# One transformer-like layer on one core: queries and keys split at the input projection, attention's output halves added by a transfer

## The chip, the cores and the metric

The kernel runs on 1 core of one Trainium2 chip. The metric is the device time of one execution in microseconds (us). Engines are named as in the profile: PE is TensorE's matmul, PEld its weight load, DVE is VectorE, ACT is ScalarE, POOL is GpSimd, SP is SyncE, which here only issues transfers.

## The reference, cut to what matters

One layer on x (2048 x 1024): a normalisation, one input projection of 2816 columns, two groups of heads (sliding-window attention with sinks, and a gated linear recurrence), an output projection, cross-attention into 256 memory tokens, and a SwiGLU network. The change touches the projection's first 640 columns and the attention:

```python
u = rms_norm(h, g_mix_pre[l])
z = u @ w_in[l]
qa, ka, va, qh, fh, ih, gh = jnp.split(z, IN_SPLITS, axis=-1)     # 512, 128, 128, 512, 512, 512, 512
...
s = jnp.einsum('bnqhgd,bnkhd->bhgqk', qc, kband).astype(jnp.float32) * (Dh ** -0.5)
s = jnp.where(valid[None, :, None, None, None, :], s, NEG_INF)
sink = jnp.broadcast_to(sinks.astype(jnp.float32).reshape(1, 1, Hkv, G, 1, 1), (B, NC, Hkv, G, CHUNK, 1))
p = jax.nn.softmax(jnp.concatenate([s, sink], axis=-1), axis=-1)[..., :L]
o = jnp.einsum('bnhgqk,bnkhd->bnqhgd', p.astype(v.dtype), vband)
```

There are 8 query heads and 2 key and value heads of 64, a window of 128 frames in chunks of 64, and Dh ** -0.5 = 0.125.

## The kernel before

**Precision.** Every f32 product is made of parts: an operand x becomes hi, x rounded to f32r by a copy, and lo = x - hi. A product is three matmuls, hi*hi + hi*lo + lo*hi (`mm3`, L156 to L158). A split is a copy on ACT (L999) or POOL (L1001) and a subtraction on DVE (L1002).

**Stages.** First (0 to about 265 us), `in_first` reads x, normalises it, transposes it and multiplies it with the input projection's weights for the first 1024 frames. It goes over pairs of column blocks of 128. Pairs are either plain (`in_block` with plain, columns 4, 5 and 0, 1; three matmuls for each product, result in tiles zp, copied by ACT L654 and stored) or made by a scheme with seven products for a 2 x 2 block (`seven`, L1162 to L1164), whose products are copied out of PSUM to tiles part (ACT L1177) and added by DVE (L661) into a tile z of two columns. Tiles zp, th and part come from one pool with three buffers (tag "part"). The blocks 2 and 3 are the first that go through the seven products. The steps run in the order 1, 5, 6, 3, 7, 2, 4; the steps 1, 6, 7 and 4 use one PSUM bank, so the copy of step 1's product must be done before step 6 can begin. z goes to DRAM as z_d, columns by frames; columns 0 to 511 are the queries, 512 to 639 the keys, 640 to 767 the values. At the end `in_first` also multiplies the first pair (columns 4, 5) for frames 1024 to 2047; the other columns of these frames are made by `in_cols`, one column of 128 at a time, beside the attention.

**Attention** (about 265 to 610 us) goes over 16 tiles of 128 frames, each in two methods. `swa_front` loads the queries of four heads twice into qd, rows 0 to 63 and 64 to 127 (64 rows are one head's dimension), so that the upper half can become hi and the lower half lo of the same numbers: ACT L787 scales by -0.125, DVE L788 makes the lower half the difference. Keys are loaded twice into kr and split by POOL (kh, L1001) and DVE (kl, L1002). The products with the queries are L822 and L823: 128 rows carry hi and lo of q at once. DVE L827 adds the mask and takes the minimum (w_mn), ACT L831 the exponential, POOL L834 and L837 the sink's part of the sum (w_se, w_dn), DVE L839 the reciprocal (w_rd) and L842 the scaling of the rows S. `swa_back`, a tile later, transposes S on PE (L856), splits it (pth by ACT L860, ptl by DVE L861), and multiplies with the stacked v (vst: 64 columns hi, 64 columns lo; L865, L866). The bank's lower and upper 64 rows then hold two halves of the output, which are added: ACT L869 copies one into ys, DVE L870 adds the other. SP stores ys into y_d[n, :, 0:512]. ys has one buffer. Beside this run the recurrence's tiles (`hgrn`) and the remaining columns of the projection, both of which put matmuls between those of attention. Everything from about 640 us on is the same in both kernels.

**Order.** The program is written as generators that take turns; a scheduler with a simulated timeline sets the order of instructions on each engine, and each engine then runs its own in that order. An instruction that waits holds up everything behind it on its engine. All transfers of this part are issued by SP. Transfers that add into DRAM, issued by POOL, are there in the network's last stage already (`add_to`, L1566, y_d<-row).

## Time and profile before

| | |
|---|---|
| median of 3 runs | 2534.37 us (2533.18 to 2536.8) |
| profiled execution, span | 2530.8 us, 34134 instructions |
| PE busy | 2496.8 us, 99% |
| DVE busy | 1794.5 us, 71% |
| ACT busy | 1262.1 us, 50% |
| POOL busy | 375.2 us, 15% |
| DMA | 470.07 MB in 305133 packets, 186 GB/s in the mean |

The profiled execution's own time isn't given beside its span; the median stands 3.57 us above the span, for what lies around it. An engine's busy time counts its instructions; idle time is put down to what released the instruction that ended it. "x32" counts instructions, "us to landing" is from a transfer's issue to the end of its write. A slow clock of PE shows as PEclk below 1.00. PE is nearly always busy, so what counts is what PE waits for, stage by stage.

### The profile page before, as it was taken

Reading aid. Unit: us, or ns where it says so; the run is one execution under the profiler, and the core shown is the slowest. Engines: PE = TensorE matmul, PEld = TensorE weight load, DVE = VectorE, ACT = ScalarE, POOL = GpSimd, SP = SyncE. Lnnn points to the kernel's source line nnn. Section 1 sums busy time; section 2 is a strip of 40 time slices with the busy share of each in tenths; the row PEclk is TensorE's granted clock in tenths of the full one; section 3 lists DMA queues with packets and bytes.
Section 4 is the critical chain, followed back from the end, with each engine's and each line's share of the span. In section 5 each row is a group of like instructions: output and inputs, shape, how many; then the busy total and the mean of one; then the engine's idle time right before and its main releaser. Section 6 shows DMA issues by size and latency. Waiting matters only on the chain.

```text
span 2530.8 us, 34134 instructions
## 1 busy us (share of the span) xinstructions
PE 2496.8 (99%) x11942; PEld 2087.0 (82%) x11942; DVE 1794.5 (71%) x2863; ACT 1262.1 (50%) x2627; POOL 375.2 (15%) x540
## 2 busy tenths in 40 slices
PE   9999999999999999999999999999999999999998
PEld 8878888888987888878878888888888888888886
DVE  8785488986557889988866655576566557664766
ACT  5453466655565576566753333353333335443543
POOL 4231344321401111112200000000000000000022
PEclk9999999999999999999999999999999999999999
DMA  6455645673887996758944322254354334565776
GB/s 199 152 167 177 176 145 156 199 248 114 276 311 261 299 335 196 251 175 256 346 161 168 135 77 93 80 192 154 129 208 167 117 130 155 182 178 112 228 173 153
DMA packets 305133, 470.07 MB, mean 186 GB/s; under 512 B 21440, under 2 KB 193472, under 8 KB 304960
## 3 DMA queue, kind: packets, MB, share of 16 engines
q1 hardware_dynamic: 298912, 445.86, 52.7%
q0 software_dynamic: 6048, 22.02, 5.1%
q8 instruction: 94, 1.54, 0.3%
q14 instruction: 79, 0.65, 0.1%
HBM read 301.09 MB, written 166.72 MB: 185 GB/s over the span
## 4 chain that ended last, share of the span: by engine, by line
PE 84%; DVE 6%; DMA 4%; ACT 3%; issue 2%; POOL 1%; SPq 0%; DVEq 0%; POOLq 0%; ACTq 0%
PE psm L1164 23%; PE psm L1162 23%; PE psm L1163 22%; PE psg L156 2%; PE psg L158 2%; PE psg L157 2%; DVE T L1002 1%; DVE S L1002 1%; DMA raw<-in_wo_x_dram 1%; ACT junk L1533 1%; SPq L75 0%; DMA row<-h_d 0%; PE pss L156 0%; PE pss L157 0%; PE pss L158 0%
## 5 line engine op out<-in xcount | busy, mean ns | idle before, releaser
L1162 PE MATMUL psm<-T,S 128*128 128x512 f32 x2680 | 1034.3, 391 | 10.3 <-ACT part L1177 5.6
L1163 PE MATMUL psm<-T,S 128*128 128x512 f32 x2680 | 1042.9, 390 | 1.5 <-DVE T L1002 1.4
L1164 PE MATMUL psm<-T,S 128*128 128x512 f32 x2680 | 1029.8, 390 | 3.7 <-DVE S L1002 3.7
L1162 PEld LDWEIGHTS psm<-T,S 128*128 128x128 f32 x2680 | 503.2, 188 | 122.5 <-ACT part L1177 9.9
L1164 PEld LDWEIGHTS psm<-T,S 128*128 128x128 f32 x2680 | 503.4, 188 | 111.1 <-DVE S L1002 6.7
L1163 PEld LDWEIGHTS psm<-T,S 128*128 128x128 f32 x2680 | 503.5, 188 | 107.2 <-DVE T L1002 3.7
L999 ACT ACTIVATE S<-sum 128x512 fp32r<-128x512 f32 (+1 forms) x370 | 224.3, 620 | 375.7 <-PE psm L1164 274.2
L1002 DVE TENSOR_TENSOR S<-sraw,S 128x512 fp32r<-128x512 f32 (+1 forms) x315 | 212.1, 680 | 237.2 <-ACT S L999 234.1
L1177 ACT ACTIVATE part<-psm 128x512 f32<-128x512 f32 x285 | 168.8, 597 | 260.4 <-PE psm L1164 241.9
L1002 DVE TENSOR_TENSOR S<-sum,S 128x512 fp32r<-128x512 f32 (+1 forms) x388 | 258.5, 675 | 45.2 <-ACT S L999 41.2
L999 ACT ACTIVATE S<-sraw 128x512 fp32r<-128x512 f32 (+1 forms) x300 | 184.4, 618 | 109.2 <-PE psm L1164 107.3
L1566 POOL DMA_DIRECT2D y_d<-row x16 | 14.1, 879 | 1077.0 <-DVE row L1748 1026.1
L1002 DVE TENSOR_TENSOR T<-row,T 128x1024 fp32r<-128x1024 f32 (+1 forms) x112 | 131.0, 1186 | 27.7 <-ACT T L999 25.7
L156 PE MATMUL psg<-u,whi 128*128 128x512 f32 x320 | 127.6, 399 | 1.3 <-DVE z L730 1.3
L158 PE MATMUL psg<-u,wlo 128*128 128x512 f32 x320 | 127.4, 399 | 0.0
L157 PE MATMUL psg<-u,whi 128*128 128x512 f32 x320 | 127.4, 398 | 0.0
L1533 ACT ACTIVATE junk<-row 128x512 f32<-128x512 f32 x160 | 99.7, 625 | 43.5 <-DVE row L1555 21.2
L999 ACT ACTIVATE T<-row 128x1024 fp32r<-128x1024 f32 (+1 forms) x112 | 113.4, 1032 | 7.3 <-DMA row<-in_w_down_dram 2.8
L1699 DVE TENSOR_TENSOR row<-psm,part 128x512 f32<-128x512 f32 x66 | 44.1, 688 | 71.3 <-PE psm L1164 71.3
L1002 DVE TENSOR_TENSOR wlo<-raw,whi 128x1024 fp32r<-128x1024 f32 x52 | 64.0, 1232 | 41.4 <-ACT whi L999 30.6
L1748 DVE TENSOR_TENSOR row<-psm,part 128x512 f32<-128x512 f32 x72 | 49.2, 689 | 49.3 <-PE psm L1164 49.1
L831 ACT ACTIVATE S<-S,w_mn 128x256 f32<-128x256 f32 (+1 forms) x128 | 63.1, 496 | 41.4 <-DVE w_mn L827 41.0
(355 smaller groups left out, 3541.3 us busy)
## 6 DMA issues: line engine op xcount, KB each, us to landing
sraw<-in_w_gate_dram SPq DMA_DIRECT2D x44, 512.0 KB, 3.8
sraw<-in_w_up_dram SPq DMA_DIRECT2D x44, 512.0 KB, 3.7
hid_d<-row SPq DMA_DIRECT2D x44, 512.0 KB, 2.7
sraw<-hid_d SPq DMA_DIRECT2D x32, 512.0 KB, 4.4
sraw<-in_w_in_dram SPq DMA_DIRECT2D x48, 256.0 KB, 3.8
z_d<-pair SPq DMA_DIRECT2D x20, 512.0 KB, 3.3
raw<-in_w_in_dram SPq DMA_DIRECT2D x20, 512.0 KB, 4.6
z_d<-z SPq DMA_DIRECT2D x20, 512.0 KB, 3.8
```

Source lines behind the costliest of these rows:

```text
L156: nc.tensor.matmul(ps, ah, bh, start=(i == 0), stop=False)
L157: nc.tensor.matmul(ps, ah, bl, start=False, stop=False)
L158: nc.tensor.matmul(ps, al, bh, start=False, stop=(i == n - 1))
L831: nc.scalar.activation(s[:, r, o:], s[:, r, o:], AF.Exp, bias=mn[:, i:i + 1], scale=-1.0, accum_out=den[:, i:i + 1])
L999: self.nc.scalar.activation(hi, raw, AF.Copy)
L1002: self.nc.vector.tensor_tensor(lo, raw, f32(hi), ALU.subtract)
L1162: nc.tensor.matmul(ps, s[:, 0, k, :], t[:, 0, k, :], start=st, stop=False, **kw)
L1163: nc.tensor.matmul(ps, s[:, 0, k, :], t[:, 1, k, :], start=False, stop=False, **kw)
L1164: nc.tensor.matmul(ps, s[:, 1, k, :], t[:, 0, k, :], start=False, stop=sp, **kw)
L1177: nc.scalar.activation(t, ps, AF.Copy)
L1533: self.nc.scalar.activation(junk, a, AF.Square, scale=float(D) ** -0.5, accum_out=to)
L1748: nc.vector.tensor_tensor(d, a, b, ALU.add)
```

## The change

Queries and keys leave the input projection's PSUM banks already split, in two new tensors in DRAM: zq_d (2 x 512 x 2048, scaled by -0.125) and zk_d (2 x 128 x 2048). `halved_store` does it: ACT copies the bank, scaled, to hi; DVE makes lo = bank * f - hi in one instruction; two stores. It stands in the plain blocks (two zp tiles for a column instead of one, out of the same three buffers), in the block of columns 2 and 3 (one more pair of tiles), at the end of `in_first`, and in `in_cols` for columns 0 to 3. `swa_front` then loads the parts where they are wanted: qs directly (four buffers), and kh and kl in one tile kk (two buffers). The scaling, the difference of q and the split of k in each tile go. v's split takes one instruction on ACT and one on DVE instead of two and two. In `swa_back` ACT copies the whole bank of each pair of heads to ys, the addition on DVE goes; SP stores rows 0 to 63 of ys into y_d, and POOL then issues a second transfer of rows 64 to 127 that adds into the same place.

```diff
+    def halved_store(self, c0, t0, src, hi, lo):
+        nc = self.nc
+        dst, r, f = (self.zq_d, c0, -0.125) if c0 < C_KA else (self.zk_d, c0 - C_KA, 1.0)
+        n = hi.shape[1]
+        nc.scalar.activation(hi.bitcast(F32R), src, AF.Copy, scale=f)
+        nc.vector.scalar_tensor_tensor(lo.bitcast(F32R), src, f, hi, ALU.mult, ALU.subtract)
+        for e, t in enumerate((hi, lo)):
+            self.store(dst[e, r:r + P, t0:t0 + n], t)
...
             if plain:
-                self._n += 1
-                t = self.st_pool.tile([P, 512], F32, tag="part", name=f"zp_{self._n}", bufs=3)
-                nc.scalar.activation(t, a, AF.Copy)
-                self.store(self.z_d[c0:c0 + P, j * 512:(j + 1) * 512], t)
+                t = []
+                for e in range(2 if c0 < C_VA else 1):
+                    self._n += 1
+                    t.append(self.st_pool.tile([P, 512], F32, tag="part", name=f"zp_{self._n}", bufs=3))
+                if c0 < C_VA:
+                    self.halved_store(c0, j * 512, a, *t)
...
-            qd = ph.tile([P, 4, P], F32, tag="qd", name=f"qd{n}_{g}", bufs=2)
-            qsrc = z[g * 256:(g + 1) * 256, t0:t0 + P].rearrange("(h d) t -> d h t", d=64)
-            self.load(qd[0:64], qsrc)
-            self.load(qd[64:128], qsrc)
-            q = ph.tile([P, 4, P], F32R, tag="qs", name=f"qs{n}_{g}", bufs=2)
-            nc.scalar.activation(q, qd, AF.Copy, scale=-0.125)
-            nc.vector.scalar_tensor_tensor(q[64:128], qd[64:128], -0.125, f32(q[64:128]), ALU.mult, ALU.subtract)
+            q = ph.tile([P, 4, P], F32R, tag="qs", name=f"qs{n}_{g}", bufs=4)
+            for e in range(2):
+                self.load(f32(q[64 * e:64 * e + 64]),
+                          self.zq_d[e, g * 256:(g + 1) * 256, t0:t0 + P].rearrange("(h d) t -> d h t", d=64))
...
-        self.split(kr[:, :, o:], kh[:, :, o:], kl[:, :, o:])
+        for e in range(2):
+            self.load(f32(kk[64 * e:64 * e + 64, :, :, o:]).rearrange("d e g t -> d (e g) t"),
+                      self.zk_d[:, :, t0 + P - nk * P:t0 + P].rearrange("e (g d) t -> d (e g) t", d=64))
...
-            nc.scalar.activation(ys[a], pr[c], AF.Copy)
-            nc.vector.tensor_tensor(ys[a], pr[a], ys[a], ALU.add)
-        self.store(self.y_d[n, :, 0:512], ys.rearrange("p k t -> p (k t)"))
+            nc.scalar.activation(ys[:, g, :], ps, AF.Copy)
+        dst = self.y_d[n, :, 0:512].rearrange("(g d) c -> d g c", g=2)
+        self.store(dst, ys[0:64])
+        nc.gpsimd.dma_start(dst, ys[64:128], accum_op=ALU.add)
```

What moves with it is shown by the engines' orders, where lines of the change have their own numbers (the seven products' copy is L1177 before and L1204 after, the split's copy L999 and L1026). Numbers behind a name tell tiles apart and differ between the kernels.

ACT about 60 to 75 us, at the end of the plain columns 0 and 1 and the beginning of the block of columns 2 and 3; before:

```order
L654 ACTIVATE zp_712<-psm_665 128x512
L654 ACTIVATE zp_727<-psm_666 128x512
L999 ACTIVATE T_738<-pair_117 128x1024 x2
L1177 ACTIVATE part_761<-psm_748 128x512
L999 ACTIVATE S_835<-sraw_662 128x512
L1177 ACTIVATE part_795<-psm_782 128x512
L1177 ACTIVATE part_814<-psm_748 128x512
```

and with the change:

```order
L642 ACTIVATE zp_726<-psm_679 128x512
L642 ACTIVATE zp_744<-psm_680 128x512
L1026 ACTIVATE T_758<-pair_119 128x1024 x2
L1026 ACTIVATE S_860<-sraw_676 128x512
L1204 ACTIVATE part_781<-psm_768 128x512
L1204 ACTIVATE part_815<-psm_802 128x512
L1026 ACTIVATE S_907<-sraw_762 128x512
```

The copy of the first product (part_761, now part_781) stands behind one split more, and the buffers that it and the two tiles zp take are now shared with the differences of these columns.

DVE at the same place; before:

```order
L446 SCALAR_TENSOR_TENSOR pair_770<-pair_770,n_r_934,g_113 128x1024
L1137 TENSOR_TENSOR sum_890<-sraw_742,sraw_745 128x512
L1002 TENSOR_TENSOR T_696<-pair_119,T_696 128x1024 x2
L1431 STREAM_TRANSPOSE pair_770<-pair_770 128x512 x2
L1137 TENSOR_TENSOR sum_916<-sum_890,sraw_742 128x512
L1002 TENSOR_TENSOR T_738<-pair_117,T_738 128x1024 x2
L1137 TENSOR_TENSOR sum_954<-sraw_745,sum_916 128x512
L1002 TENSOR_TENSOR S_835<-sraw_662,S_835 128x512
L1002 TENSOR_TENSOR S_851<-sraw_662,S_851 128x512
```

and with the change:

```order
L1029 TENSOR_TENSOR T_710<-pair_121,T_710 128x1024
L1164 TENSOR_TENSOR sum_926<-sraw_762,sraw_765 128x512
L1029 TENSOR_TENSOR T_710<-pair_121,T_710 128x1024
L643 SCALAR_TENSOR_TENSOR zp_727<-psm_679,zp_726 128x512
L448 SCALAR_TENSOR_TENSOR pair_790<-pair_790,n_r_970,g_115 128x1024
L1164 TENSOR_TENSOR sum_952<-sum_926,sraw_762 128x512
L1029 TENSOR_TENSOR T_758<-pair_119,T_758 128x1024 x2
L643 SCALAR_TENSOR_TENSOR zp_745<-psm_680,zp_744 128x512
L1029 TENSOR_TENSOR S_860<-sraw_676,S_860 128x512
```

The difference zp_727, to be stored before its buffer can be used again, stands between the splits of T and a scaling of x (L448, L446 before) that was ahead of them; zp_745 follows four rows on.

POOL in the third tile of attention; before:

```order
L834 TENSOR_TENSOR w_se_2680<-sink,w_mn_2658 128x4
L907 TENSOR_TENSOR q_3078<-qq_3063,G 128x512
L837 TENSOR_TENSOR w_dn_2683<-w_den_2659,w_se_2680 128x4
L1001 TENSOR_SCALAR kh_2892<-kr_2890 128x512
L947 TENSOR_SCALAR h_vv_2771<-h_ss_2765 128x4
L930 TENSOR_TENSOR W_3053<-W_2776,G 128x512
L949 TENSOR_TENSOR h_rs_2773<-h_vv_2771,mhalf 128x4
L834 TENSOR_TENSOR w_se_2713<-sink,w_mn_2691 128x4
L837 TENSOR_TENSOR w_dn_2716<-w_den_2692,w_se_2713 128x4
```

and with the change:

```order
L862 TENSOR_TENSOR w_se_2949<-sink,w_mn_2927 128x4
L898 DMA y_d<-ys_2752 64x2x512
L934 TENSOR_TENSOR q_3368<-qq_3353,G 128x512
L865 TENSOR_TENSOR w_dn_2952<-w_den_2928,w_se_2949 128x4
L974 TENSOR_SCALAR h_vv_3068<-h_ss_3062 128x4
L976 TENSOR_TENSOR h_rs_3070<-h_vv_3068,mhalf 128x4
L862 TENSOR_TENSOR w_se_2982<-sink,w_mn_2960 128x4
L865 TENSOR_TENSOR w_dn_2985<-w_den_2961,w_se_2982 128x4
L957 TENSOR_TENSOR W_3343<-W_3073,G 128x512
```

The split of k (kh) is gone, and the adding transfer of the first tile's ys stands between the two halves of a sink's sum (w_se, w_dn). It waits for the store of the other half of ys.

ACT at the end of attention, from the last copies of tile 14 to those of tile 15 (ys is one buffer, so a tile's first copy waits until the tile before has left it); before:

```order
L860 ACTIVATE pth_11_6287<-pst_6282 128x512
L869 ACTIVATE ys_6247<-psh_6266 64x512
L860 ACTIVATE pth_00_6371<-pss_6366 128x512
L860 ACTIVATE pth_01_6380<-pst_6375 128x512
L869 ACTIVATE ys_6247<-psh_6291 64x512
L860 ACTIVATE pth_10_6396<-pss_6391 128x512
L860 ACTIVATE pth_11_6405<-pst_6400 128x512
L904 ACTIVATE atz_2376<-pst_6491 64x2x64
L869 ACTIVATE ys_6365<-psh_6384 64x512
L869 ACTIVATE ys_6365<-psh_6409 64x512
```

and with the change:

```order
L888 ACTIVATE pth_10_6135<-pss_6130 128x512
L895 ACTIVATE ys_6105<-psh_6124 128x512
L888 ACTIVATE pth_11_6144<-pst_6139 128x512
L888 ACTIVATE pth_00_6228<-pss_6223 128x512
L1026 ACTIVATE whi_6503<-raw_6501 128x1024
L758 ACTIVATE z_6279<-psg_6307 128x512
L888 ACTIVATE pth_01_6237<-pst_6232 128x512
L931 ACTIVATE atz_2416<-psg_6342 64x2x64
L888 ACTIVATE pth_10_6252<-pss_6247 128x512
L895 ACTIVATE ys_6105<-psh_6148 128x512
```

The two copies of tile 14 (ys_6105) have eight rows from one to the other where they had three.

55 lines of the change are left out of this document (35 added, 20 removed).

## The prediction

> **What bounds the kernel now.** I read the page's first part, then a table of stretches, then TensorE's waits in the stage that the change edits. First the span, and the one engine that fills it:
>
> ```profile
> span 2530.8 us, 34134 instructions
> PE 2496.8 (99%) x11942; PEld 2087.0 (82%) x11942; DVE 1794.5 (71%) x2863; ACT 1262.1 (50%) x2627; POOL 375.2 (15%) x540
> ```
>
> PE idles 2530.8 - 2496.8 = 34 us in all. The change adds no matmul and removes none that counts, so it can only move those 34 us, the stretches at a lower granted clock, and new waits. Work taken off DVE, ACT and POOL is worth what PE waited for it. The stretches of the sliding attention (265 to 610 us) say how much that is; columns are busy time of PE, its weight load, DVE, ACT and POOL, then the granted clock, DMA share and GB/s:
>
> ```profile
> 265.00:300.00 35.00, 34.05 (x179) 28.93 (x178) 18.63 (x56) 14.99 (x54) 13.20 (x19) 0.95 0.69 196
> 380.00:400.00 20.00, 19.54 (x120) 16.87 (x118) 17.21 (x48) 13.28 (x46) 8.81 (x13) 1.00 0.56 173
> 400.00:420.00 20.00, 19.66 (x119) 16.87 (x118) 19.75 (x43) 16.16 (x42) 10.38 (x15) 1.00 0.51 162
> 500.00:520.00 20.00, 18.69 (x96) 15.53 (x95) 16.57 (x38) 8.73 (x24) 2.42 (x4) 1.00 0.98 348
> 520.00:580.00 60.00, 60.00 (x315) 50.52 (x314) 55.27 (x138) 37.46 (x111) 18.48 (x31) 1.00 0.59 197
> 580.00:610.00 30.00, 28.28 (x152) 23.34 (x151) 23.56 (x63) 19.04 (x46) 2.06 (x6) 0.94 0.41 124
> ```
>
> PE's idle time in the stage is 0.95 + 0.46 + 0.34 + 1.31 + 1.72 = 4.8 us, and the lower clock costs 5% of 35 us and 6% of 30 us, 1.75 + 1.8 us: **8.3 us is all that this stage has to give**, out of 345. The waits of PE there name the edited lines:
>
> ```profile
> PE psg L156 <- DVE z L730: 1.3, 1, 1.3
> PE pst L823 <- DVE kl L1002: 0.8, 1, 0.8
> PE psh L865 <- DVE ys L870: 0.8, 1, 0.8
> PE pss L856 <- DVE w_mn L827: 0.8, 1, 0.8
> ```
>
> All four are DVE being late. Two are instructions that the change removes (kl, the addition into ys), two stand behind DVE's queue.
>
> **What is removed.** The groups of the stage, with busy time and mean ns:
>
> ```profile
> L788 DVE SCALAR_TENSOR_TENSOR qs<-qd,qs 64x512 fp32r<-64x512 f32 x32 | 25.8, 809 | 21.1 <-ACT qs L787 20.2
> L787 ACT ACTIVATE qs<-qd 128x512 fp32r<-128x512 f32 x32 | 19.6, 627 | 10.4 <-DMA qd<-z_d 5.0 <-PE psh L823 2.1 <-DMA raw<-in_w_in_dram 1.8
> L1001 POOL TENSOR_SCALAR kh<-kr 128x512 fp32r<-128x512 f32 (+1 forms) x16 | 12.7, 796 | 31.8 <-PE pst L823 16.8 <-DMA g<-in_g_mix_post_dram 6.0 <-PE psh L822 3.9
> L1002 DVE TENSOR_TENSOR kl<-kr,kh 128x512 fp32r<-128x512 f32 (+1 forms) x16 | 11.6, 728 | 1.9 <-POOL kh L1001 1.7
> L870 DVE TENSOR_TENSOR ys<-psh,ys 64x512 f32<-64x512 f32 x16 | 11.0, 687 | 1.6 <-ACT ys L869 1.3
> ```
>
> With the other 16 additions at the same 0.69 us, DVE loses 25.8 + 11.6 + 22 = 59 us, ACT 20, POOL 13. Only the 8.3 us above can come back from it. Stretch by stretch: in 265 to 300 the wait for kl goes, and with it perhaps the slow window after it; 2.0 of 2.7 us. In 380 to 420, 0.8 us go: DVE is busy for 19.75 of the second 20 us and loses 59/16 = 3.7 us for each tile of attention. At 500, 1.3 us: the line waited for is not edited, but it stands in the same queue. In 580 to 610 one of the two 0.8 us waits is the addition itself, the other is a softmax row behind it; there the new transfers also stand in the way (below), so I take 0.5 of 3.5. Together **-4.6 us, between 0 and -8.3**. Next late after the removed stalls is ACT, whose copy of ys now frees the bank alone, in the same 0.59 us as before.
>
> **What is added before attention.** Twenty differences on DVE and twenty scaled copies on ACT. Their nearest row, the same operation on the same shape and source:
>
> ```profile
> L730 DVE SCALAR_TENSOR_TENSOR z<-z,psg 128x512 f32<-128x512 f32 x13 | 8.8, 676 | 0.1
> ```
>
> Twelve of these fall before 265 us and eight beside attention, where 59 us were taken off. The copies mostly take the place of copies that were there. What counts is the first 80 us, where DVE has no gap:
>
> ```profile
> 63.00:73.00 10.00, 10.00 (x46) 8.28 (x45) 10.00 (x13) 6.00 (x10) 2.17 (x2) 1.00 0.60 176
> 42.92 0.19 PEld L1163 LDWEIGHTS psm<-u,S 128*128 128x128 f32 x1 [0.26 <-DVE u L1002]
> ```
>
> The second row is TensorE already waiting for DVE's last piece of u. The first new difference now stands ahead of that on DVE; instructions of this size follow each other at 0.61 us (the next rows, 63.06 to 63.67), so TensorE comes **0.6 us** later.
>
> The other early term is a buffer. Tiles zp and part share one pool of three. A column block written in two parts takes two of them, and the second is filled by DVE and sent last. The copy of the seven-product block's first product (part, L1177, after the change L1204) now needs the buffer of the difference zp_727, and so its landing. In the profile of before that copy waited for nothing of the kind:
>
> ```profile
> 66.88 0.60 ACT L1177 ACTIVATE part<-psm 128x512 f32<-128x512 f32 x1 [0.22 <-ACT T L999]
> 63.06 0.68 DVE L1002 TENSOR_TENSOR S<-sum,S 128x512 fp32r<-128x512 f32 x1
> 63.67 1.27 DVE L446 SCALAR_TENSOR_TENSOR pair<-pair,n_r,g 128x1024 f32<-128x1024 f32 x1
> 64.86 0.68 DVE L1137 TENSOR_TENSOR sum<-sraw,sraw 128x512 f32<-128x512 f32 x1
> 65.46 2.35 DVE L1002 TENSOR_TENSOR T<-pair,T 128x1024 fp32r<-128x1024 f32 x2
> 67.74 0.70 DVE L1431 STREAM_TRANSPOSE pair<-pair 128x512 f32<-128x512 f32 x1
> 69.35 0.39 PE L1162 MATMUL psm<-T,S 128*128 128x512 f32 x1
> DMA to landing us min/median/max: 2.7/2.7/2.7
> ```
>
> In the new order of DVE, zp_727 follows the pair of splits of T at 65.46, that is at 67.74, less the scaling of 1.19 us (63.67 to 64.86) that now comes after it, plus four earlier differences of 0.61 us: it starts at 69.0 and ends at 69.7. The two stores of zp in this place (last row) landed 2.7 us after their issue, so the buffer is free at 72.4 and the copy, 0.60 us, done at 73.0. TensorE needs the bank that this copy frees for its sixth product, in before at 69.35; two matmuls of another product now go first (0.46 us) and it is 0.6 us late, so it would start at 70.4. It stands for **2.6 us**. All eight stores of zp landed in 2.4 to 7.7 us, so this term lies between 0 (DVE runs ahead of my count) and 7.6 us.
>
> A stall costs a second time through the clock:
>
> ```profile
> 275.00:278.00 3.00, 2.05 (x15) 1.45 (x12) 2.97 (x5) 0.89 (x4) 2.46 (x3) 1.00 0.32 91
> 278.16:281.57 3.41, 3.41 (x10) 2.63 (x10) 3.29 (x17) 2.64 (x13) 0.20 (x1) 0.50 0.83 281
> ```
>
> After 0.95 us of idle time in 3 us, the clock was halved for 3.41 us, which costs 1.7 us. I take 0.6 of that, 1.0 us, for the stall at 70. The Trainium skill ("TensorE: Matmul & The Clock Gate", Part 1) says that a free-running window of about 3.4 us has to be idle before the clock drops; by that rule 2.6 us of waiting would bring no slow window and the sum would be 1.0 us lower. The row differs: less than a third of the time before the drop was idle.
>
> Early cost: 0.6 + 2.6 + 1.0 = **+4.2 us**, between +0.6 and +9.9. Later copies that share the pool with a late store are costed at nothing: between the end of a product and the next write of its bank TensorE runs another product of the seven (66.63 to 69.35 in the rows above, some 2.7 us). Where that cover is too short, the price is again what a landing has left over, as in the 2.6.
>
> **What is added in attention.** The loads of q move the same bytes as before, one load for each of the two parts instead of two loads of the same rows; k's two loads carry twice the bytes. All stand in SP's queue with the stores of the halves. The scaled copy of q idled 5.0 us in 32 instructions for these loads (row of L787), and TensorE waited for none of them, so I cost them at 0, and up to +1.3 us at 500, where the DMA engines are at 0.98 and the wait there would simply change its name. The 32 additions into ys become 16 transfers with an accumulate, which POOL issues. Nearest rows: the same kind of transfer later in the kernel, twice the bytes, and the present store of ys:
>
> ```profile
> y_d<-row POOLq DMA_DIRECT2D x16, 512.0 KB, 5.4
> y_d<-ys SPq DMA_DIRECT2D x16, 256.0 KB, 3.9
> L1566 POOL DMA_DIRECT2D y_d<-row x16: 856/865/1110, 2237.0 to 2373.6; - x16
> ```
>
> So 0.87 us of POOL each, 14 us in all, about what kh gave back, and each waits for the store's landing (2 to 4 us), with the softmax's w_se and w_dn behind it on POOL, for which DVE's reciprocal waits. Of TensorE's waits none names POOL or the rows scaled with the reciprocal, so there is lead between them, and I cost POOL's wait at 0; without that lead each of the 16 would cost up to the 3.9 us of a landing. Its effect near the end is in the 0.5 above.
>
> **Sum.** 2530.8 + 4.2 - 4.6 = 2530.4 of span. The median of the three runs, 2534.37, stands 3.57 above the profiled span; with that, **2534**.
>
> **Rivals.**
> 1. The forecast: early cost and gain cancel, 2534; its own range is 2530 to 2538.
> 2. Faster: DVE was the whole trouble, all 8.3 us go, and DVE reaches zp_727 early enough. 2534.4 - 8.3 + 0.6 = 2526.7. For it: every wait listed names DVE. Against it: DVE is full in 63 to 73.
> 3. Slower: the single buffer of ys. There is one, and a tile's first copy into it now waits for the accumulate of the tile before, not for its store alone. From issue of the store that is 3.9 + 0.87 + up to 5.4 = 10.2 us. What the kernel leaves today, from store to next copy:
>
> ```profile
> 559.00 0.57 SPq L78 DMA_DIRECT2D y_d<-ys  x1
> 565.94 0.60 ACT L869 ACTIVATE ys<-psh 64x512 f32<-64x512 f32 x1
> 592.83 9.67 SPq L78 DMA_DIRECT2D y_d<-ys  x2
> 597.18 0.59 ACT L869 ACTIVATE ys<-psh 64x512 f32<-64x512 f32 x1
> ```
>
> That is 6.9 us for one tile and 4.4 us near the end: ACT would stand 3.3 and 5.8 us there, with the copies of the next probabilities queued behind it, on which the products with v wait. If two such waits reach TensorE less 2 us of lead each (1.3 + 3.8), each with a slow window (3.4), and the last stretch gains nothing (0.5), the time is 2534 + 9 = 2543. It decides where the accumulate lands more than 2 us after the copy's turn. Against it: the new order on ACT puts more instructions between the two halves of the late tiles. The Trainium skill ("SBUF — State Buffer", "The 'DVE blocks DMA' trap") adds that a GpSimd-issued transfer can be held until a DVE instruction gives up a shared port, which would lengthen this. The row of L1566 (at most 1.11 us, beside a busy DVE) shows no such thing.
> 4. The change does nothing for TensorE: its waits in attention were of order, others take their place. 2534.4 + 4.2 = 2538.6.
>
> **How the numbers follow.** Chances 0.42, 0.15, 0.28, 0.15. I count as no change whatever is within 0.2%, 5 us, about what a measurement of this kernel can tell. Faster: rival 2 and a tail of the first, 0.18. Slower: rival 3 and half of the tail of 4, 0.31. The range reaches from rival 2 to a little past rival 3: 2526.5 to 2545.
>
> **What would show it.** In the profile after: PE waits for ACT's part (L1204) near 70 us by 2 to 3 us, the clock perhaps 0.5 behind it; no wait for kl or ys; DVE some 55 us less in 265 to 610. Rival 3 shows as ACT idle before ys (L895), released by a DMA to y_d. I am wrong if PE idles in attention for more than 5 us, or if nothing stands at 70.

## The result, and the profile after

| | before | after |
|---|---|---|
| median (range), 7 runs each on one chip | 2536.8 us (2533.18 to 2541.83) | **2546.48 us** (2543.51 to 2547.04) |
| ratio of the two, 95% interval | | **1.0038** [1.0028, 1.0049] |
| profiled execution, span | 2530.8 us | 2544.0 us |

The change costs 9.7 us. The forecast was 2534 us with a range up to 2545, so the time lies 1.5 us outside it. Of the 12.5 us between the forecast and the measured time, 2.4 are the base: the median of before was 2534.37 us in three runs and is 2536.8 in these seven. The two profiled executions lie 13.2 us apart, more than the medians, since one execution of a kernel differs from another (8.7 us from the lowest to the highest run of before, 3.5 of the changed kernel). Before attention two kernels below that are the same as before up to there (e8, e9) come to its end within 0.3 us of before's trace. With the change the spread there is wider: e6, e11 and e12 run the same instructions in the same order up to attention and come to it 4.65, 6.54 and 8.66 us late, e4 and e10 likewise 9.22 and 7.62. So a difference of some 4 us between two traces tells nothing by itself.

The first part of the page of the changed kernel:

```profile
span 2544.0 us, 33974 instructions
PE 2498.6 (98%) x11942; PEld 2086.2 (82%) x11942; DVE 1745.2 (69%) x2787; ACT 1241.7 (49%) x2582; POOL 360.9 (14%) x540
```

As many matmuls, DVE 49 us less, ACT 20 and POOL 14 us less, and still the span is longer. PE now idles 2544.0 - 2498.6 = 45.4 us, where it had idled 34.

First the stage that the change was costed to help. The windows of attention in the changed kernel (columns as in the prediction):

```profile
265.00:300.00 35.00, 35.00 (x171) 29.33 (x170) 10.29 (x27) 8.01 (x24) 10.04 (x13) 1.00 0.88 258
380.00:400.00 20.00, 20.00 (x117) 17.34 (x116) 15.45 (x43) 11.55 (x41) 8.32 (x12) 1.00 0.68 190
400.00:420.00 20.00, 20.00 (x126) 17.74 (x125) 13.10 (x32) 13.76 (x40) 9.89 (x15) 1.00 0.76 175
500.00:520.00 20.00, 20.00 (x105) 16.88 (x104) 18.30 (x43) 11.13 (x33) 6.86 (x11) 1.00 1.00 308
520.00:580.00 60.00, 58.12 (x304) 48.44 (x303) 37.99 (x106) 28.57 (x87) 14.38 (x25) 1.00 0.82 249
580.00:610.00 30.00, 30.00 (x161) 25.41 (x160) 20.91 (x63) 18.80 (x54) 5.77 (x13) 1.00 0.54 146
```

PE is full in five of the six stretches and the clock is 1.00 in all. Its waits of at least 0.2 us from 265 to 620 us in the changed kernel (what it waited for; us in total, times, longest):

```profile
PE psh L850 <- ACT ys L895: 0.9, 1, 0.9
PE psh L893 <- ACT pth L888: 0.8, 1, 0.8
PE psh L894 <- DVE ptl L889: 0.2, 1, 0.2
```

The waits for z, kl and w_mn are gone. So attention did what was hoped. The loss stands ahead of it. The windows of the three early stretches and of attention, before:

```profile
0.00:100.00 100.00, 96.28 (x518) 83.02 (x519) 78.33 (x102) 51.25 (x89) 38.91 (x57) 1.00 0.63 190
100.00:150.00 50.00, 47.56 (x208) 38.40 (x207) 46.66 (x61) 32.85 (x50) 21.79 (x25) 1.00 0.44 136
150.00:265.00 115.00, 113.55 (x500) 93.35 (x499) 72.77 (x105) 43.91 (x69) 26.89 (x36) 1.00 0.53 177
265.00:620.00 355.00, 350.22 (x1957) 300.62 (x1955) 291.14 (x705) 215.74 (x622) 116.38 (x178) 0.99 0.55 176
```

and the same with the change:

```profile
0.00:100.00 100.00, 92.31 (x499) 78.94 (x500) 82.98 (x110) 51.17 (x88) 35.16 (x55) 1.00 0.64 198
100.00:150.00 50.00, 40.79 (x159) 31.77 (x158) 33.08 (x45) 23.46 (x35) 14.75 (x20) 0.90 0.37 112
150.00:265.00 115.00, 111.88 (x490) 91.25 (x489) 85.04 (x117) 53.40 (x83) 25.32 (x36) 1.00 0.51 167
265.00:620.00 355.00, 352.79 (x1970) 302.80 (x1969) 233.40 (x617) 190.87 (x569) 111.00 (x184) 1.00 0.76 213
```

The number behind each busy time counts instructions. PE does 19, 49 and 10 matmuls fewer in the three early stretches; matmuls follow each other there at 0.228 us, so that is 4.3, 11.2 and 2.3 us of work left behind. The stretch from 100 to 150 us is the worst, and in it *DVE is less busy than before* (33.08 against 46.66 us): it is not overloaded there, it waits too.

A second measure puts one number on each stage. The matmuls of the seven-product scheme are as many in both traces and run in nearly the same order; the delay of the n-th of them is its start after the change less the start of the n-th one before. This **delay** is +1.7 us at 46 us of before's time, +4.3 at 71 and still 4.3 shortly ahead of 100, 6.2 at 105, 12.0 at 110, 15.7 at 126, and **17.65 us** from 177 us to the last one before attention (960th, at 232 us). The first one behind attention (1010th, 765 us) is 11.67 us late, so attention and what lies beside it gave back 6.0. The last is 13.3 us late.

### The profile page after: what moved, and what is told of

It reads as the page before. It is cut to its first block, busy times and chain, and to the rows that moved or that the text cites. A ratio compares the mean times of both kernels' runs of the same rounds, so it can differ in the third digit from the quotient of the medians.

```text
span 2544.0 us, 33974 instructions
## 1 busy us (share of the span) xinstructions
PE 2498.6 (98%) x11942; PEld 2086.2 (82%) x11942; DVE 1745.2 (69%) x2787; ACT 1241.7 (49%) x2582; POOL 360.9 (14%) x540
## 4 chain that ended last, share of the span: by engine, by line
PE 83%; DVE 6%; DMA 4%; issue 3%; ACT 3%; POOL 1%; SPq 0%; DVEq 0%; ACTq 0%; POOLq 0%
PE psm L1191 22%; PE psm L1189 22%; PE psm L1190 22%; PE psg L157 2%; PE psg L158 2%; PE psg L156 2%; DVE S L1029 1%; DVE T L1029 1%; DMA raw<-in_wo_x_dram 1%; ACT junk L1560 1%; DMA pair<-in_x_dram 1%; DMA u_d<-row 1%; DVE sum L1164 1%; PE pss L156 0%; PE pss L158 0%
## 5 line engine op out<-in xcount | busy, mean ns | idle before, releaser
L1026 ACT ACTIVATE S<-sum 128x512 fp32r<-128x512 f32 (+1 forms) x370 | 224.3, 620 | 382.7 <-PE psm L1191 271.5
L1204 ACT ACTIVATE part<-psm 128x512 f32<-128x512 f32 x285 | 168.3, 597 | 264.0 <-PE psm L1191 235.0
L1026 ACT ACTIVATE S<-sraw 128x512 fp32r<-128x512 f32 (+1 forms) x300 | 184.5, 618 | 116.3 <-PE psm L1191 114.3
L1026 ACT ACTIVATE T<-row 128x1024 fp32r<-128x1024 f32 (+1 forms) x112 | 113.4, 1032 | 8.1 <-DMA row<-d_s 3.9
L1164 DVE TENSOR_TENSOR sum<-sraw,sraw 128x512 f32<-128x512 f32 (+1 forms) x97 | 65.6, 677 | 20.6 <-DMA sraw<-in_w_in_dram 13.3
```

Of the source, the lines that this page charges most:

```text
L1026: self.nc.scalar.activation(hi, raw, AF.Copy)
L1164: nc.vector.tensor_tensor(t, a, b, op)
L1204: nc.scalar.activation(t, ps, AF.Copy)
```

## Where the early time goes, read from the trace

TensorE's rows at its waits from 40 to 140 us in the changed kernel (start, length, what it runs, and in brackets the idle time before it and what ended that):

```profile
44.60 0.50 PE L1190 MATMUL psm<-u,S 128*128 128x512 f32 x1 [1.58 <-DVE u L1029]
71.54 0.50 PE L1189 MATMUL psm<-u,S 128*128 128x512 f32 x1 [0.35 <-ACT S L1026]
73.98 0.50 PE L1189 MATMUL psm<-T,S 128*128 128x512 f32 x1 [1.71 <-ACT part L1204]
110.80 0.50 PE L1189 MATMUL psm<-T,S 128*128 128x512 f32 x1 [1.62 <-DVE pair L690]
114.95 0.50 PE L1189 MATMUL psm<-u,S 128*128 128x512 f32 x1 [1.09 <-ACT S L1026]
119.32 0.79 PE L1191 MATMUL psm<-u,S 128*128 128x512 f32 x1 [3.63 <-DVE S L1029]
139.78 0.50 PE L1189 MATMUL psm<-T,S 128*128 128x512 f32 x1 [2.20 <-DVE pair L690]
```

The first three rows stand at the two places that the prediction counted. The four behind them are not in it: 8.5 us of waiting, with DVE the releaser of three. To see why DVE is late, follow it back. Its timeline with the change:

```profile
70.13 0.68 DVE L643 SCALAR_TENSOR_TENSOR zp<-psm,zp 128x512 fp32r<-128x512 f32 x1
...
78.20 1.27 DVE L1029 TENSOR_TENSOR S<-sraw,S 128x512 fp32r<-128x512 f32 x2
...
88.30 0.69 DVE L1164 TENSOR_TENSOR sum<-sraw,sraw 128x512 f32<-128x512 f32 x1 [3.72 <-DMA sraw<-in_w_in_dram]
...
97.18 1.27 DVE L1029 TENSOR_TENSOR S<-sraw,S 128x512 fp32r<-128x512 f32 x2
...
108.86 1.28 DVE L448 SCALAR_TENSOR_TENSOR pair<-pair,n_r,g 128x1024 f32<-128x1024 f32 x1 [8.41 <-POOL n_r L104]
```

and the same work before (an x2 or x3 merges rows that follow each other):

```profile
72.82 1.88 DVE L1002 TENSOR_TENSOR S<-sraw,S 128x512 fp32r<-128x512 f32 x3
...
89.06 1.55 DVE L1002 TENSOR_TENSOR S<-sraw,S 128x512 fp32r<-128x512 f32 x2
```

The split of the raw weights (S<-sraw) ends at 79.5 where it ended at 74.7. It reads their buffer last, and before, the load of the next weights waited for it: SP stood for 3.2 us, until the end of a split released it at 74.13. SP's queue with the change:

```profile
79.97 0.95 SPq L75 DMA_DIRECT2D sraw<-in_w_in_dram  x2
...
99.11 1.30 SPq L75 DMA_DIRECT2D sraw<-in_w_in_dram  x2
100.45 0.68 SPq L75 DMA_DIRECT2D pair<-in_x_dram  x1
```

and before:

```profile
74.16 0.95 SPq L75 DMA_DIRECT2D sraw<-in_w_in_dram  x2
...
90.67 1.01 SPq L75 DMA_DIRECT2D sraw<-in_w_in_dram  x2
91.74 0.50 SPq L75 DMA_DIRECT2D pair<-in_x_dram  x1
```

The loads go out 5.8 us late, then 8.4, and the load of x, which stands in the queue behind the second, 8.7. With the change SP comes to these loads of weights from stores (un_d<-pair, zq_d<-pair) that had themselves waited for DVE's transposes (L1458), until 77.71 and 96.09 us; the last of the stores is out at 79.46 and 99.01, about when the splits end (79.5 and 98.5). Either way the queue waits for DVE, and the trace doesn't part the two ways. Between them DVE idles 3.72 us for the first weights (88.30), which makes the next split late, and so the next load: the delay goes round. The ring ends at x, whose norm on ACT began at 96.74 us before:

```profile
96.74 1.06 ACT L444 ACTIVATE pair<-pair 128x1024 f32<-128x1024 f32 x1 [0.89 <-DMA pair<-in_x_dram]
```

and with the change only at 106.77 (second row):

```profile
73.33 0.60 ACT L1204 ACTIVATE part<-psm 128x512 f32<-128x512 f32 x1 [1.85 <-DVE sum L1164]
...
106.77 1.06 ACT L446 ACTIVATE pair<-pair 128x1024 f32<-128x1024 f32 x1 [7.05 <-DMA sraw<-in_w_in_dram]
```

ACT idles 7.05 us. The profile names the load of weights there, but the load of x landed at 106.70, 0.07 us ahead of the norm and 10.0 us later than before (96.71). DVE behind it idles 8.41 us (108.86), and then all that TensorE needs comes at once out of two engines that are both behind: the waits at 110 to 119. Then the clock. Windows of the changed kernel in the two places:

```profile
119.00:122.00 3.00, 2.68 (x6) 2.15 (x7) 3.00 (x5) 0.00 (x0) 1.55 (x3) 0.50 0.00 0
...
140.00:143.00 3.00, 3.00 (x10) 2.34 (x10) 3.00 (x4) 0.91 (x2) 1.48 (x3) 0.65 0.41 165
```

Matmuls that follow each other at 0.23 us do so at 0.43, ten from 119.3 to 123.8 and eight from 140.8 to 144.1, which costs 3.6 us. Waiting (9.2 us of idle time from 100 to 150, where it was 2.4) and clock make 10.4 of that stretch's 11.2.

**Theory A**: this ring, fed by the six added differences of the plain columns 4, 0 and 1 (six instructions at 0.61 us while DVE has no gap) and by the buffers that their second tiles take. **Rivals**: B, the four differences and eight stores of the block 2 and 3, which stand in DVE's and SP's queues at 83 to 98 us, are to blame; C, the place of the stores in SP's queue ahead of the loads is; D, the single buffer of ys is.

## The experiments

Each row's ratio is to runs of the kernel before, made beside it on the same chip. "Before attention" is the delay of the 960th matmul of the scheme, "in attention" the change of the delay from there to the 1010th (minus is a gain); both are from one profiled execution.

| kernel | median us | ratio [95%] | delay before attention | in attention |
|---|---|---|---|---|
| after | 2546.48 | 1.0038 [1.0028, 1.0049] | 17.65 | -6.0 |
| e1 block 2, 3 undone | 2549.21 | 1.0052 [1.0034, 1.0071] | 15.85 | -0.3 |
| e2 block's stores late | 2540.05 | 1.0016 [1.0005, 1.0027] | 9.23 | -4.5 |
| e3 block without lo | 2541.2 | 1.0022 [1.0013, 1.0032] | 13.49 | -5.6 |
| e4 five buffers | 2536.39 | 1.0006 [0.9995, 1.0016] | 9.22 | -7.2 |
| e5 e4, plain without lo | 2530.65 | 0.9979 [0.9969, 0.9988] | 3.95 | -6.4 |
| e6 e4, x loaded by POOL | 2534.81 | 0.9994 [0.9984, 1.0004] | 4.65 | -6.6 |
| e7 e4 and e2 | 2537.74 | 1.0004 [0.9995, 1.0013] | 9.95 | -6.4 |
| e8 adding transfer alone | 2544.41 | 1.0031 [1.0022, 1.0041] | 0.28 | +10.7 |
| e9 e8, two ys | 2538.43 | 1.0013 [1.0004, 1.0022] | 0.23 | +4.3 |
| e10 e4 without adding transfer | 2534.25 | 0.9998 [0.9989, 1.0008] | 7.62 | -8.4 |
| e11 e6 without adding transfer | 2531.66 | 0.9987 [0.9978, 0.9996] | 6.54 | -8.5 |
| e12 e6, two ys | 2530.64 | 0.9985 [0.9976, 0.9995] | 8.66 | -10.5 |
| e13 plain columns undone | 2535.8 | 0.9993 [0.9983, 1.0003] | 1.57 | -0.1 |
| e14 first half undone | 2532.61 | 0.9985 [0.9976, 0.9994] | -0.10 | -0.8 |
| e15 e12, six pair tiles | 2532.77 | 0.9985 [0.9976, 0.9995] | 10.39 | -10.1 |

### e1_undo23: columns 2 and 3 of the first half as before

```diff
-            if c0 < C_VA:
+            if c0 < 0:
...
+            if n < NPB and g == 1:
+                qd = ph.tile([P, 4, P], F32, tag="qd", name=f"qd{n}_{g}", bufs=2)
+                self.load(qd[0:64], qsrc)
+                self.load(qd[64:128], qsrc)
```

> Only the block of columns 2 and 3 is undone: it leaves the projection whole, as before, and the first eight tiles split these four heads' queries themselves. If the loss of 17.7 us before attention comes from this block's added work (four differences on DVE, eight stores instead of two), it falls to the 4.3 us that were lost before the block ends (1.7 at the first u, 2.6 at the buffer of zp_727), and the time is about 2546.5 - 13 = 2533 to 2535. If the six differences of the plain columns 4, 0 and 1 alone make DVE late enough, more than 10 of the 17.7 us stay and the time is 2541 or more.

15.85 of the 17.65 us stay. The split of the weights still ends at 77.9 and the next one at 94.3, and TensorE still waits 3.6 us for S. Rival B falls as the main cause. And attention gains nothing in this execution, though only the second four heads of half the tiles went back; this reappears in e13 and e14.

### e2_late_stores: the block's parts stored where z was stored

```diff
-                self.halved_store(c0, j * 512, a, hi, lo)
+                self.halved(c0, a, hi, lo)
...
+            if not plain and c0 < C_VA:
+                for i, c in enumerate((ca, cb)):
+                    for e in range(2):
+                        self.store(self.zq_d[e, c * P:(c + 1) * P, 0:TB], z[1 - e][:, i, :])
```

> The same work as the changed kernel, but the parts of columns 2 and 3 are stored once, whole rows of 1024, at the place where the block was stored before: four stores instead of eight, in another place of SP's queue. Theory queue (the stores wait for DVE's differences on SP, ahead of the loads of weights and x): the loads that went from 90.7 to 99.1 us come back, 10 us or more are won, 2534 to 2537. Theory DVE (DVE is late, and its split of the weights frees their buffer late): the loads stay where they are, at most 2 us are won, 2544 to 2547.

9.23 instead of 17.65: the place of eight stores in SP's queue (four longer ones here) is worth up to 8 us as long as the rest is late. The median came out between the two forecasts. The load of x still goes out 7.7 us late, at 99.48, as theory DVE had it; at 115 us of before's time the delay is 9.1 instead of 12.9, and from there it grows by 0.2 us instead of 4.8. Alone this speaks for rival C; e7 tells how far it goes.

### e3_no_lo23: the block without its differences

```diff
-                self.halved_store(c0, j * 512, a, hi, lo)
+                nc.scalar.activation(hi.bitcast(F32R), a, AF.Copy, scale=-0.125)
+                for e in range(2):
+                    self.store(self.zq_d[e, c0:c0 + P, j * 512:(j + 1) * 512], hi)
```

> Leaves out the four differences of columns 2 and 3 on DVE (the copy is stored in place of the difference, so those four heads' scores lack the low part for the first 1024 frames); stores, buffers and copies as in the changed kernel. Theory DVE: four instructions of 0.61 us less ahead of the weights' split, and no store waits for them: 5 to 10 us less than the changed kernel, 2537 to 2541. Theory queue: the eight stores still stand ahead of the loads, but wait for ACT only, so nearly all of it is won as well; the two differ by what e2 shows. If neither is right: 2545 or more.

Four DVE instructions less in this block return 4.2 of 17.65 us. That is hardly more than two executions can differ by, and the intervals of the two medians overlap. These differences may share in the delay; they do not make it.

### e4_part5: five buffers instead of three for zp, th and part

```diff
-                    t.append(self.st_pool.tile([P, 512], F32, tag="part", name=f"zp_{self._n}", bufs=3))
+                    t.append(self.st_pool.tile([P, 512], F32, tag="part", name=f"zp_{self._n}", bufs=5 if self.raws == 3 else 3))
```

> The pool of zp and part has five buffers instead of three in the first stage. The stall of 2.6 us at 72 us (ACT's copy of the first product waits for a store's landing) should go. If it is a loss by itself: 2544, 2 to 3 us less than the changed kernel, the loss from 105 to 150 us unchanged. If it starts the later losses (ACT held, so weights split late): 2534 to 2538.

TensorE has no wait left from 60 to 85 us: the stall of the prediction was the buffer. Half of the loss goes (17.65 to 9.22, and 7.62 in e10, which is the same up to there). What stays is one wait of 1.36 us at 97 and one of 3.98 at 114, behind the ring: the load of x goes out at 98.67, 7 us later than before, and ACT waits for it:

```profile
104.07 1.06 ACT L446 ACTIVATE pair<-pair 128x1024 f32<-128x1024 f32 x1 [4.77 <-DMA pair<-in_x_dram]
```

### e5_p5_no_lo_plain: e4, the plain columns without their differences

```diff
-                    self.halved_store(c0, j * 512, a, *t)
+                    nc.scalar.activation(t[0].bitcast(F32R), a, AF.Copy, scale=f)
+                    for e in range(2):
+                        self.store(dst[e, r:r + P, j * 512:(j + 1) * 512], t[0])
```

> Five buffers as in e4, and leaves out the six differences of the plain columns 4, 0 and 1 on DVE (the copy is stored in place of the difference, so these queries and keys lack their low part for the first 1024 frames); the number of stores is the same. Theory plain: these six instructions make DVE's splits of the weights late in the first 80 us, so that the next loads of weights and of x are issued 6 to 8 us late on SP. Then the loads come back to about 91 us, and the 7 us that e4 still loses from 96 to 115 us fall below 2; 2529 to 2533. If they are not the cause: as e4, 2535 to 2538.

With buffers in plenty, the six differences (3.7 us of DVE at 0.61) are still worth 5.3 us of delay (3.7 against e10), and in the medians 0.27% or some 7 us, clear of the intervals. More than their own length: the part that theory A claims. Stores and bytes are those of e4; but a column here also takes one buffer instead of two, and its stores wait for ACT alone, which this run doesn't part from the differences.

### e6_p5_x_pool: e4, the load of x issued by POOL

```diff
-                self.load(t[:, 0, :], self.I["x"][TB + n * P:TB + (n + 1) * P, :])
+                nc.gpsimd.dma_start(t[:, 0, :], self.I["x"][TB + n * P:TB + (n + 1) * P, :])
```

> Five buffers as in e4, and the loads of x that stand beside the projection are issued by POOL instead of SP. In e4 DVE stands for 3.7 us, and ACT for 4.8, for a row of x whose load was issued at 98.7 us behind a load of weights that waited for its buffer. Theory queue: POOL issues it several us earlier, that standing goes, and 3 to 6 us are won over e4: 2530 to 2534. Theory buffer: the load waits for a pair tile just the same, is issued no earlier, and the time is as e4, 2535 to 2538, or worse by what POOL then holds up.

POOL issues the load and ACT begins earlier than in e4, by 3.46 and 3.15 us:

```profile
95.21 0.60 POOL L708 DMA_DIRECT2D pair<-in_x_dram  x1
```

```profile
100.92 1.06 ACT L446 ACTIVATE pair<-pair 128x1024 f32<-128x1024 f32 x1 [4.87 <-DMA pair<-in_x_dram]
```

The delay is 4.6 us less than in e4, but this run doesn't show that the loss passes through the load. At 100 us of before's time, with x not yet waited for, 3.0 of the 4.6 are there already (-0.2 against 2.7); SP's own load of weights goes out 3.0 us earlier as well (94.47 against 97.49); e11 and e12, the same up to attention, come to 6.54 and 8.66; and the medians' intervals of e4 and e6 overlap.

The traces together say more. This load of x landed 0.4 to 1.0 us later than before in e14, e8 and e9, 2.1 in e13, 3.7 in e5, 4.2 in e6, 7.3 in e4, 8.7 in e2 and 10.0 in the changed kernel; the delay at 115 us of before's time is -0.1 to 0.3, then 1.0, 3.8, 3.3, 9.0, 9.1 and 12.9. At 100 us it had been 4.3 or less in all of these. The others lie within 3 us of the landing's lateness. So TensorE's loss from 100 to 115 us goes with the lateness of x, over kernels with different edits. Up to there the path is supported; a run that moves x alone, and by more than the spread, is missing.

### e7_p5_late: e4 and e2 together

> Five buffers and the late, whole stores of columns 2 and 3 together. If the two gains were of different losses (e4 won 10 us, e2 6 us of the changed kernel), up to 14 us are won: 2532. If they took away the same loss after 120 us, as their traces suggest: as e4, 2535 to 2537.

9.95 against 9.22 in e4 and 9.23 in e2: the two do not add. With five buffers the place of the block's stores costs nothing that these runs can see, so rival C is not shown to be a cause of its own; e2 helped where the stores stood behind a queue that was late already.

### e8_acc_only: the kernel before with the adding transfer and v's split alone

```diff
-        ys = ph.tile([P, 4, P], F32, tag="ys", name=f"ys{n}")
+        ys = ph.tile([P, 2, 512], F32, tag="ys", name=f"ys{n}")
...
-        self.store(self.y_d[n, :, 0:512], ys.rearrange("p k t -> p (k t)"))
+        dst = self.y_d[n, :, 0:512].rearrange("(g d) c -> d g c", g=2)
+        self.store(dst, ys[0:64])
+        nc.gpsimd.dma_start(dst, ys[64:128], accum_op=ALU.add)
```

> The kernel of before with one part of the change alone: the two halves of the output added by POOL's transfer, and v's split in two instructions. Theory of the prediction: DVE's additions cost TensorE 0.8 us and a share of the waits behind them, so 1 to 4 us are won in attention, 2531 to 2533. Theory of the single buffer: ACT waits for the accumulate of the tile before, and 2 to 9 us are lost, 2537 to 2543.

A surprise: alone this part is nearly as dear as the whole change, 0.31% (2544.41 us, above the 2543 expected at most), and all of it in attention, +10.7 us. Its window, and TensorE's longest waits there:

```profile
265.00:620.00 355.00, 343.39 (x1906) 291.24 (x1905) 268.03 (x649) 207.46 (x601) 130.84 (x193) 1.00 0.65 184
```

```profile
PE pss L855 <- DVE w_mn L826: 2.9, 2, 1.8
PE psh L864 <- ACT pth L859: 2.4, 2, 1.5
```

PE idles 11.6 us where it idled 4.8, behind softmax rows and pth, the copies that the prediction's third rival put in ACT's queue behind ys. Four of ACT's copies into ys begin 0.07 to 0.08 us after the landing of an adding transfer (at 454.80, 513.68, 605.58 and 616.18 us), the second and the last after 3.63 and 3.87 us of idle time.

### e9_acc_ys2: e8 with two buffers of ys

```diff
-        ys = ph.tile([P, 2, 512], F32, tag="ys", name=f"ys{n}")
+        ys = ph.tile([P, 2, 512], F32, tag="ys", name=f"ys{n}", bufs=2)
```

> e8 (the adding transfer alone, 8 to 11 us lost in attention) with two buffers for ys instead of one. Theory of the single buffer: ACT no longer waits for the accumulate of the tile before, and at least half of the loss goes, 2535 to 2540. Theory POOL (what costs is POOL held at the accumulate for the store's landing, with the softmax's sums behind it) or order (the transfers moved the softmax among the other instructions): the time stays at 2542 to 2546.

```profile
265.00:620.00 355.00, 348.04 (x1946) 296.46 (x1945) 270.79 (x656) 210.08 (x606) 132.89 (x195) 1.00 0.65 186
```

6.4 of the 10.7 us come back, 40 matmuls more in the window, and no copy into ys that waited begins at a landing any more. So the third rival is real, in a kernel where attention still splits q and k; how much of the 6.4 is those waits and how much the order of instructions, which is another from about 530 us on, isn't parted. The other 4.3 us are not the buffer; what they are stays open. A candidate that no run tests is POOL, whose wait at the adding transfer the prediction costed at 0: DVE's reciprocal (w_rd) waits 18.1 us for POOL's sum (w_dn) in e8 and 18.7 in e9, from 265 to 620 us, where it waited 8.3 before.

### e10_p5_no_acc and e11_p5_x_no_acc: e4 and e6 with ys added on DVE as before

```diff
-            nc.scalar.activation(ys[:, g, :], ps, AF.Copy)
-        self.store(dst, ys[0:64])
-        nc.gpsimd.dma_start(dst, ys[64:128], accum_op=ALU.add)
+            nc.scalar.activation(ys[a], pr[c], AF.Copy)
+            nc.vector.tensor_tensor(ys[a], pr[a], ys[a], ALU.add)
```

> e4 (the changed kernel with five buffers) without the adding transfer and with v's split as before: queries and keys split at the projection alone. If the transfer costs the same in the whole change as alone (e8: 8 to 11 us), this is 2525 to 2529. If the waits of attention have only 8.3 us to give in all, as the prediction counted, and e4 has had 7 of them, it is at most 2 us faster than e4: 2533 to 2537.

> e6 (five buffers, x loaded by POOL beside the projection) without the adding transfer. 1 to 2 us below e6 if little is left in attention (2532 to 2535), 5 or more if the transfer costs there what it costs alone (2524 to 2529).

Attention gains 1.2 and 1.9 us more without the adding transfer than with it (-8.4 against -7.2, -8.5 against -6.6), less than executions differ by, and in the medians the intervals overlap both times. In the changed kernel the transfer is at most a small cost.

### e12_p5_x_ys2: e6 with two buffers of ys

> e6 with two buffers for ys. In the changed kernel ACT waits 6.4 us for transfers of ys, in two waits. If such a wait reaches TensorE, 1 to 3 us are won over e6, 2531 to 2534; if not, as e6, 2534 to 2536.

```profile
265.00:620.00 355.00, 355.00 (x2008) 306.95 (x2007) 236.85 (x625) 196.20 (x582) 112.25 (x182) 1.00 0.75 211
```

TensorE does not wait once in attention. All of the stage's reserve is taken, 10.5 us in this execution (the delay is read from 232 to 765 us, so it takes in more than the 265 to 610 us of the prediction's 8.3), and the kernel is faster than before by 0.15%.

### e13_undo_plain: columns 0, 1 and 4 of the first half as before

```diff
-                for e in range(2 if c0 < C_VA else 1):
+                for e in range(1):
...
-                if c0 < C_VA:
-                    self.halved_store(c0, j * 512, a, *t)
-                else:
-                    nc.scalar.activation(t[0], a, AF.Copy)
-                    self.store(self.z_d[c0:c0 + P, j * 512:(j + 1) * 512], t[0])
+                nc.scalar.activation(t[0], a, AF.Copy)
+                self.store(self.z_d[c0:c0 + P, j * 512:(j + 1) * 512], t[0])
```

> Only the plain columns 4, 0 and 1 are undone for the first 1024 frames (their tiles split these queries and keys themselves, as before); columns 2 and 3 and everything of the later frames as in the changed kernel, with three buffers. If the plain columns bring the loss before attention (theory plain), it falls from 17.7 to at most 5 us there, and what attention gains shrinks by up to the 5.7 us that e1 lost by its undoing: 2531 to 2540. If block 2, 3 brings it, together with anything else, more than 10 us stay: 2544 or more.

This is the decisive one, the counterpart of e1: with the plain columns' six differences, second tiles and added stores out and the block 2, 3 left in, the delay is 1.57 us, not 17.65. SP's queue is nearly that of before,

```profile
75.05 0.95 SPq L75 DMA_DIRECT2D sraw<-in_w_in_dram  x2
...
93.00 0.94 SPq L75 DMA_DIRECT2D sraw<-in_w_in_dram  x2
```

0.9 and 2.3 us late instead of 5.8 and 8.4, and TensorE's worst stretch is nearly that of before too, 204 matmuls where before has 208 and the change 159:

```profile
100.00:150.00 50.00, 46.63 (x204) 37.62 (x202) 45.48 (x61) 32.67 (x51) 20.93 (x27) 1.00 0.43 131
```

### e14_undo_first: e13, and the block 2, 3 undone too

> Everything before attention undone; only the frames from 1024 on are split at the projection. Before attention the loss should be within 1 us of none. Attention then gains for eight of its sixteen tiles: 0 to 4 us by the prediction's sum, 2531 to 2536; if the adding transfer costs there what it costs alone, 2538 to 2546.

No delay before attention, so what is left of the change costs no time there. The median is 0.15% under before's.

### e15_best_pair6: e12 with six tiles for pairs instead of five

```diff
-        return self.st_pool.tile([P, 2, D], F32, tag="pair", name=f"pair_{self._n}", bufs=5)
+        return self.st_pool.tile([P, 2, D], F32, tag="pair", name=f"pair_{self._n}", bufs=6)
```

> e12 with six pair tiles instead of five in the first stage. If the load of x still waits for a tile there, 2 to 4 us less than e12: 2527 to 2529. If the loads wait for DVE only: as e12, 2529 to 2532.

The same ratio as e12, so a sixth tile brings nothing that the medians show. Its trace tells no more: 6.6 us of the delay stand before 46 us already here, with an order of instructions of its own.

## Why the prediction was wrong, step by step

**What bounds the kernel**: right. TensorE idles for DVE, and only its waits count.

**From span to time, 3.57**: not all of it lies around the span. The changed kernel's seven runs stand 1.7 us above their own spans; the rest says that the profiled execution of before was a fast one.

**Gain in attention, -4.6 (0 to -8.3)**: right in sign and about in size, -6.0 by the delay. DVE fell by 291.14 - 233.40 = 57.7 us in 265 to 620 (55 were named), the waits for z, kl and w_mn are gone, no stretch has a slow clock, and PE idles 2.2 us there. e4 to e6 repeat it, -6.4 to -7.2. The stretches can't be set against each other one by one, since the changed kernel comes to them with other work.

**First u, 0.6**: too small in this execution. TensorE waited 1.58 us (44.60), and the delay there is 1.67. In e1 to e4, e6, e7 and e10 to e12, which keep these differences, it is -0.2 to 1.5, with 0.6 in the middle.

**The buffer of zp_727, 2.6**: right. The difference began at 70.13 (69.0 was worked out), the copy of part at 73.33 (72.4), 2.5 us behind the difference's end, and the delay grows there by 4.30 - 1.67 = 2.63. The profile puts the copy down to an addition on DVE; but the store of the difference, issued at 70.83, landed at 73.26, 0.07 us ahead of the copy, and five buffers in e4 take the wait away.

**Half clock behind it, 1.0**: not there. After 2.06 us of waiting the matmuls went on at full rate.

**The sum of the early cost, +4.2**: at 80 us it was right, 4.3, by luck: one term was too small and one too large. **This is the step that failed: it stopped there.** "What counts is the first 80 us", and "later copies that share the pool with a late store are costed at nothing". From 100 to 177 us another 13.3 us were lost. Two things went wrong in it. The cover of 2.7 us, another product of the seven, was taken to hold for each later step, though DVE came out of the first 80 us about 5 us late and stayed so; that is read from the rows, and no run takes it by itself. And DVE was followed only to the instructions that wait for its results, not to the transfers: the stores that wait for its transposes, the buffer of raw weights that its splits free, and the loads that stand behind both in SP's queue. e13 and e1 put the loss on the plain columns' part of the change, e4 on the buffers for about half, e5 on the differences (with a buffer for each) for most of the rest. The path through the load of x is supported by its landing in all the kernels (under e6), not by a run that moves it alone and clearly. The prediction's two signs of being wrong, PE idling for more than 5 us in attention or nothing standing at 70, both stayed away: they looked only where the sum had counted.

**Loads and stores in SP's queue, 0**: no run shows a cost of their number or bytes (e7 for the block's stores; none of TensorE's waits in attention names a load). Wrong in that the queue hands on a lateness: x stood behind stores and weights that were late.

**Third rival, ys**: its price was about right, its reach not. The wait came about where it was put, at the last tile, on ACT in the changed kernel:

```profile
622.30 1.09 ACT L895 ACTIVATE ys<-psh 128x512 f32<-128x512 f32 x2 [5.53 <-DMA y_d<-ys]
```

5.53 us, where 5.8 had been worked out; but PE is busy for 10.00 of the 10 us from 620 to 630, so it reached no matmul. A second, 4.54 us of idle time, ends at 515.49, 0.07 us behind a landing; PE is full there too (500 to 520). In all of attention TensorE waited 0.9 us for ys. Without the relief of attention the adding transfer costs 10.7 us (e8), of which a second buffer returns 6.4 (e9). The argument against it, more instructions between the two halves, is tested by no run. That this rival's time, 2543, lies near the measured one is luck: the loss stands ahead of attention.

**What stays open**: the 4.3 us of e9; how the loss of the first stage divides between late stores, late splits and the load of x; why executions of one order differ by up to 4 us there (e6, e11, e12); and why attention gains next to nothing when part of the first half's queries or keys goes back (e1, e13, e14: -0.1 to -0.8, against -6.0), more than the share of work that goes back. Each is one execution, and the scheduler orders each kernel anew.

## What to carry to other kernels

When instructions are added to an engine with no gap, follow not only who waits for its results but which buffers it is the last to read, and which load stands behind each buffer on an issuing queue: six added DVE instructions, 3.7 us of work, with the six buffers that their results take became 16 us here (17.65 against 1.57), along with two rounds of late loads. A cover that is read from the old trace ("another product runs meanwhile") holds only while the covering work itself is on time, so a sum has to run to the place where the late engine next idles of itself. And two parts of a change can carry each other: the adding transfer cost 0.31% alone and nothing that the medians can tell beside the part that emptied DVE.

## What the runs showed of the hardware

A transfer that adds into DRAM landed later here than a store of the same 256 KB. In the changed kernel, attention's two transfers of ys (KB each, median us to landing):

```profile
y_d<-ys SPq DMA_DIRECT2D x16, 256.0 KB, 3.5
y_d<-ys POOLq DMA_DIRECT2D x16, 256.0 KB, 7.0
```

The prediction allowed 5.4, from the later adding transfers of twice the bytes. In e8 the same transfer took 5.0 (the store 3.6).

Of the clock: matmuls went on at full rate after waits of 0.35 and 1.71 us close together (71.54, 73.98), at half rate for 4.4 us after 1.09 and 3.63 us (114.95, 119.32), and for 3.3 us, beginning 1.0 us after the wait's end, after one of 2.20 (139.78). The Trainium skill ("TensorE: Matmul & The Clock Gate", Part 1) has the clock fall after an idle window of about 3.4 us. The first of these agrees with that. The second doesn't: the wait of 3.63 us began at 115.69, the granted clock was 1.00 from 116 to 117 us and 0.52 from 117 to 118, and PE had been busy for 0.99 us of the 3.4 from 113.60 to 117.00. Nor does the third, nor the row at 278 us of before in the prediction.
